# Lower rates for the gathered experts' steps in the dense products, and a higher one for their end

## The chip, the cores and the metric

The kernel runs on one core of a Trainium2 chip. Each of its five engines takes its instructions in order from a queue of its own: TensorE (PE) for matrix products, VectorE (DVE), ScalarE (ACT), GpSimd (POOL) and SyncE (SP), which here only issues transfers. The metric is device time in microseconds (us), the median of several runs. The profile is of one more execution, in which every instruction and transfer is recorded.

## The reference

The program is one layer of an encoder over 1024 tokens of width 1024: forgetting attention and an RWKV-7 state scan side by side, a gated merge, a layer norm, then a layer of product-key experts (PEER) and a second layer norm. The change lies in the expert layer alone:

```python
q = (xb @ w_q).reshape(t, PEER_HEADS, 2, PEER_HALF)
s = jnp.einsum('thpd,hpkd->thpk', q, sub_keys)
top_s, top_i = lax.top_k(s, K)                      # 16 of 128 keys, twice a head
...
best_s, best_pos = lax.top_k(cand_s.reshape(t, PEER_HEADS, K * K), K)
idx = jnp.take_along_axis(cand_i..., best_pos, axis=-1)
gate = jax.nn.softmax(best_s, axis=-1)
h = jax.nn.gelu(jnp.einsum('thkd,td->thk', u_table[idx], xb))
return jnp.einsum('thk,thkd->td', gate * h, v_table[idx])
```

Each token chooses 8 x 16 = 128 of 16384 experts. An expert is a row of 1024 floats of `u_table`, whose dot product with the token goes through a Gelu and is scaled by the gate, and a row of 1024 floats of `v_table`, which is added with that weight.

## The kernel before, in words

The 1024 tokens are eight tiles of 128. Two front passes of 512 tokens each do attention, scan, merge and the queries. For the expert layer the tiles are treated in two ways:

- **Gathered tiles** (0, 1, 2, 6, 7). The chosen rows of `u` are fetched one expert slot at a time: one indirect transfer on POOL's queue brings 128 rows, one for each token of the tile (`g<-u,eidx`, line 1389, tile `g`, five buffers, three ahead), and one DVE instruction makes the 128 dot products (line 1394, into `hh`). This is `experts_in`. After 128 slots come Gelu and gate, and `hh` is stored to `cijd` (line 1402). Then the `v` rows: the indices are loaded and turned by PE (`prepare`, lines 1664 to 1677), and one indirect transfer brings the 128 experts of one token (`v,ve`, line 1689) into a place, either one of seven buffers `vr` or a freed piece of the tile `C`. At most eight such rows are on their way once there are more than eight places. PE multiplies two rows at a time into `pg` with a window `win` that selects the token's line. This is the class `Rows`; a step of it uses two rows.
- **Dense tiles** (3, 4, 5). All 16384 experts are multiplied with the 384 tokens. The weight matrix `C` is built first from one-hot products, and then a loop over 128 columns of 128 experts does for column j: the hidden products of column j + 1 (`b<-x,u`, 24 matmuls), Gelu and weight (`csplit`), and the value products of column j (`v<-v,c`, 18 matmuls). A column loads 512 KB of `ut` (`uraw`) and 512 KB of `vt` (`vraw`) through SP's queue. Both are split into a high part on ACT (`uh`, `vh`) and a low part (`ul`, `vl`), of which POOL makes half and DVE half. Every four columns three transfers of 256 KB bring back pieces of `C` (`C<-cd`).

The steps of the gathered tiles are woven into PE's program when the kernel is built. Each matmul that is written "ticks" two background queues, `V` (the value steps) and `B` (top-k and dot products), with its nominal time times a rate; a queue hands out steps until its credit is used up:

```python
def tick(self, us):
    ...
    self.credit += us * self.rate
    while self.q and self.credit > 0:
        c = self._step()
        ...
        self.credit -= c
```

A dot-product slot costs 1.46 of credit, a value step 3.0; in the dense loop the value steps come in pairs (four rows for 6.0). The rates are constants: the first number of `RATEB` and `RATEV` holds while `C` is built, the second in the loop over the columns, and the third of `RATEV` from the column on in which the dot products of tile 7, the last gathered one, are done:

```python
g.B.rate, g.V.rate = RATEB[1], RATEV[1]
...
if f"g{GATHERED[-1]}" in g.B.done:
    g.V.rate = RATEV[2]
```

When the value steps of a gathered tile are done, `finals` adds them to the residual, does its layer norm and stores it, spread over some six columns. The dense tiles' norm follows the last column.

Of the kernel before, what the change touches and what calls it, by code (L numbers as in the profile page):

```python
# [27 lines left out]
TKI = 1  # L28
RATEP = (1, 1, 0.9)

RATEB = (2.1, 0.56)
RATEV = (4.2, 0.62, 0.95)
SEL = (1, 2, 3)
DENSE = (3, 4, 5)
GATHERED = (0, 1, 2, 6, 7)
# [321 lines left out]
def run(gen):  # L357
    for _ in gen:
        pass
# [1051 lines left out]
def dense_block(g, C):  # L1411
# [60 lines left out]

    g.B.rate, g.V.rate = RATEB[0], RATEV[0]
    zx = ExitStack()
# [6 lines left out]
    with tc.tile_pool(name="bp", bufs=BLEAD + 1) as bp, tc.tile_pool(name="cj", bufs=2) as cj:  # L1481
# [35 lines left out]
        run(xt)  # L1517
    g.B.rate, g.V.rate = RATEB[1], RATEV[1]
    u_hl, v_hl, c_hl, phs = {}, {}, {}, {}
# [95 lines left out]
    for j in range(128):  # L1615
# [11 lines left out]
        if f"g{GATHERED[-1]}" in g.B.done:  # L1627
            g.V.rate = RATEV[2]
        if j == 126:
# [218 lines left out]
```

## Time and profile before

| what | value |
|---|---|
| median of 3 runs | 3764.48 us (3761.63 to 3774.47) |
| the profiled execution | 3778.05 us, its span 3776.3 us |
| mean granted clock of TensorE | 0.921 |
| PE busy | 3261.2 us, 86% of the span |
| DVE, POOL, ACT busy | 2322.0, 2250.1, 1241.0 us |
| moved by transfers | 1019.61 MB, mean 270 GB/s |
| indirect transfers on POOL | 640 of `u` rows, 640 of `v` rows |

How to read it: a busy PE includes matmuls that overlap, since they are pipelined, so its share does not say how near to its peak it is. The DMA share is that of the 16 transfer engines. In rows of the windows view each stretch shows, for each engine, busy time and number of instructions. "Idle before" is time in which the engine did nothing ahead of the group named, with what ended it; "issue" stands for a wait that nothing in the profile explains. A queue's name has a q (SPq, POOLq).

### The profile page before, as it was taken

To read this page: it belongs to the slowest core of one execution; us is meant where nothing else is said; L and a number is where in the kernel's file an instruction comes from. 1 tells how busy PE (TensorE), PEld (TensorE's weight loads), DVE (VectorE), ACT (ScalarE), POOL (GpSimd) and SP (SyncE) were. 2 spreads that over 40 slices of the span, in tenths; PEclk is the share of its full clock that TensorE was granted. 3 is DMA by queue.
4 is the path that set the end of the run, shared out by engine and by line. 5 is a ranking of instruction groups with operands and counts; after the bars stand their busy time and mean duration, and the time that the engine had idled before them with its cause. 6 is when DMAs were issued, how large, how long until landed. Compare 5 with 4: busy or idle time off the path is not lost. (4 is left out here: it accounts for less than half of the span.)

```text
span 3776.3 us, 55545 instructions
## 1 busy us (share of the span) xinstructions
PE 3261.2 (86%) x20656; PEld 2345.8 (62%) x20656; DVE 2322.0 (61%) x5125; ACT 1241.0 (33%) x2530; POOL 2250.1 (60%) x1752
## 2 busy tenths in 40 slices
PE   7899999989987777777788677999888988999998
PEld 5577767865565555556533323777666766777787
DVE  3235333468898998898588753776656665632233
ACT  3442222334442121222344332333323332333343
POOL 2032125327576566777566565888878888866632
PEclk9899999999888778899899888999999999999999
DMA  4121124558787677878699999999999999999962
GB/s 141 51 90 44 50 93 148 176 163 297 234 274 243 232 251 269 297 252 280 209 389 392 347 365 366 370 367 380 382 363 396 392 373 374 384 335 371 353 214 98
DMA packets 338127, 1019.61 MB, mean 270 GB/s; under 512 B 46272, under 2 KB 84928, under 8 KB 336064
## 3 DMA queue, kind: packets, MB, share of 16 engines
q0 software_dynamic: 184320, 671.17, 48.2%
q1 hardware_dynamic: 141424, 324.11, 24.4%
q10 hardware_dynamic: 12112, 20.78, 1.5%
q8 instruction: 162, 2.65, 0.3%
q14 instruction: 109, 0.89, 0.1%
HBM read 960.81 MB, written 55.12 MB: 269 GB/s over the span
## 5 line engine op out<-in xcount | busy, mean ns | idle before, releaser
L1394 DVE CUSTOM_DVE_ANT_0 g<-g,ext 128x1024 f32<-128x1024 f32 x640 | 877.9, 1379 | 256.6 <-DMA g<-u,eidx 255.3
L1389 POOL DMA_INDIRECT g<-u,eidx x640 | 794.0, 1241 | 400.7 <-DVE hh L1394 107.9
L295 POOL TENSOR_TENSOR wl<-wraw,wh 128x1024 fp32r<-128x1024 f32 x131 | 322.9, 2465 | 503.5 <-ACT wh L294 459.8
L1689 POOL DMA_INDIRECT vr<-v,ve x430 | 463.3, 1078 | 192.6 <-issue 95.8
L277 PE MATMUL pg<-vr,win 128*32 128x512 f32 x1720 | 343.5, 638 | 81.3 <-DMA vr<-v,ve 79.1
L277 PE MATMUL b<-xh,uh 128*128 128x384 f32 x1024 | 356.8, 348 | 28.4 <-DVE C L1574 28.0
L277 PE MATMUL b<-xh,ul 128*128 128x384 f32 x1024 | 355.9, 348 | 27.7 <-POOL ul L295 27.7
L277 PE MATMUL b<-xl,uh 128*128 128x384 f32 x1024 | 354.1, 346 | 0.0
L277 PE MATMUL v<-vl,ch 128*128 128x512 f32 x768 | 308.2, 401 | 33.3 <-POOL vl L295 19.3
L294 ACT CAST wh<-wraw 128x1024 fp32r<-128x1024 f32 x150 | 157.3, 1048 | 503.8 <-PE pj L277 278.7
L277 PE MATMUL pj<-xh,wh 128*128 128x512 f32 x624 | 290.2, 465 | 20.9 <-ACT xh L294 7.0
L277 PE MATMUL v<-vh,cl 128*128 128x512 f32 x768 | 304.7, 397 | 0.0
L277 PE MATMUL v<-vh,ch 128*128 128x512 f32 x768 | 304.6, 397 | 0.0
L294 ACT CAST uh<-uraw 128x512 fp32r<-128x512 f32 x256 | 158.6, 621 | 370.0 <-PE b L277 327.5
L1689 POOL DMA_INDIRECT C<-v,ve x210 | 225.1, 1072 | 82.9 <-issue 52.1
L277 PE MATMUL pj<-xh,wl 128*128 128x512 f32 x624 | 261.4, 419 | 7.1 <-DVE wl L295 4.7
L277 PE MATMUL pj<-xl,wh 128*128 128x512 f32 x624 | 262.9, 421 | 2.3 <-DVE xl L295 2.2
L295 POOL TENSOR_TENSOR ul<-uraw,uh 128x512 fp32r<-128x512 f32 x128 | 169.3, 1323 | 152.4 <-ACT uh L294 146.3
L277 PEld LDWEIGHTS b<-xh,uh 128*128 128x128 f32 x1024 | 197.7, 193 | 57.2 <-DVE C L1574 35.4
L294 ACT CAST vh<-vraw 128x512 fp32r<-128x512 f32 x256 | 157.1, 620 | 215.4 <-PE v L277 163.9
L277 PEld LDWEIGHTS b<-xh,ul 128*128 128x128 f32 x1024 | 197.5, 193 | 47.4 <-POOL ul L295 32.9
L277 PEld LDWEIGHTS b<-xl,uh 128*128 128x128 f32 x1024 | 197.9, 193 | 20.3 <-issue 15.9
(353 smaller groups left out, 6466.2 us busy)
## 6 DMA issues: line engine op xcount, KB each, us to landing
wraw<-w SPq DMA_DIRECT2D x150, 512.0 KB, 3.4
uraw<-ut SPq DMA_DIRECT2D x128, 512.0 KB, 6.6
vraw<-vt SPq DMA_DIRECT2D x128, 512.0 KB, 6.7
cd<-S SPq DMA_DIRECT2D x12, 1344.0 KB, 8.4
C<-cd SPq DMA_DIRECT2D x63, 256.0 KB, 7.0
g<-u,eidx POOLq DMA_INDIRECT x640, 6.7
gtd<-tmp ACTq DMA_DIRECT2D x32, 256.0 KB, 2.3
g<-gtd SPq DMA_DIRECT2D x32, 256.0 KB, 3.4
```

The lines of the kernel that those rows point to most:

```text
L277: g.pe.matmul(o, l, r, start=start, stop=stop_)
L294: g.act.copy(hi, src)
L295: (lo_eng or g.dve).tensor_sub(lo, src, hi.bitcast(F32))
L1389: pool.indirect_dma_start(out=gg, out_offset=None, in_=A["u"], in_offset=bass.IndirectOffsetOnAxis(ap=idx[:, s_:s_ + 1], axis=0))
L1394: dve.tensor_tensor_reduce(out=gg, in0=gg, in1=xt, scale=1.0, scalar=0.0, op0=OP.mult, op1=OP.add, accum_out=hh[:, k:k + 1])
L1689: g.pool.indirect_dma_start(out=place, out_offset=None, in_=g.A["v"], in_offset=bass.IndirectOffsetOnAxis(ap=self.meta[i][1][:, t:t + 1], ...
```

## The change

Four numbers change. In the loop over the columns the rate of the dot products falls from 0.56 to 0.46, that of the value steps from 0.62 to 0.52, and after the last dot product the value steps' rate is 1.25 where it was 0.95.

```diff
-RATEB = (2.1, 0.56)
-RATEV = (4.2, 0.62, 0.95)
+RATEB = (2.1, 0.46)
+RATEV = (4.2, 0.52, 1.25)
```

All engines' programs are the same up to the first columns. From there the same instructions stand in other places. Three places show it.

POOL's queue in columns 88 to 90, from the low part `ul` of one column to that of the second after it (`g` rows are dot-product gathers, `vr` and `C` rows value gathers; x2 means two alike in a row). Before:

```order
L295 TENSOR_TENSOR ul<-uraw,uh 128x512
L295 TENSOR_TENSOR vl<-vraw,vh 128x512
L1689 DMA C<-v,ve 128x1024 x2
L1689 DMA vr_14988<-v,ve 128x1024
L1689 DMA vr_14989<-v,ve 128x1024
L295 TENSOR_TENSOR ul<-uraw,uh 128x512
L295 TENSOR_TENSOR vl<-vraw,vh 128x512
L1689 DMA vr_14987<-v,ve 128x1024
L1689 DMA C<-v,ve 128x1024 x3
L295 TENSOR_TENSOR ul<-uraw,uh 128x512
```

And after:

```order
L295 TENSOR_TENSOR vl<-vraw,vh 128x512
L1389 DMA g<-u,eidx 128x1024
L1689 DMA vr_14990<-v,ve 128x1024
L1689 DMA vr_14984<-v,ve 128x1024
L1689 DMA vr_14985<-v,ve 128x1024
L1689 DMA vr_14986<-v,ve 128x1024
L1389 DMA g<-u,eidx 128x1024
L295 TENSOR_TENSOR ul<-uraw,uh 128x512
L1389 DMA g<-u,eidx 128x1024
L295 TENSOR_TENSOR vl<-vraw,vh 128x512
L1389 DMA g<-u,eidx 128x1024 x2
L295 TENSOR_TENSOR ul<-uraw,uh 128x512
```

The dot products, which were done by column 84, now reach these columns, and fewer value gathers stand there.

POOL's queue in columns 112 to 114. Before:

```order
L295 TENSOR_TENSOR ul<-uraw,uh 128x512
L295 TENSOR_TENSOR vl<-vraw,vh 128x512
L295 TENSOR_TENSOR ul<-uraw,uh 128x512
L295 TENSOR_TENSOR vl<-vraw,vh 128x512
L295 TENSOR_TENSOR ul<-uraw,uh 128x512
```

And after:

```order
L295 TENSOR_TENSOR vl<-vraw,vh 128x512
L1689 DMA vr_14984<-v,ve 128x1024
L1689 DMA vr_14985<-v,ve 128x1024
L1689 DMA vr_14986<-v,ve 128x1024
L1689 DMA vr_14988<-v,ve 128x1024
L295 TENSOR_TENSOR ul<-uraw,uh 128x512
L1689 DMA vr_14989<-v,ve 128x1024
L1689 DMA C<-v,ve 128x1024 x3
L295 TENSOR_TENSOR vl<-vraw,vh 128x512
L1689 DMA C<-v,ve 128x1024 x2
L1689 DMA vr_14987<-v,ve 128x1024
L1689 DMA vr_14990<-v,ve 128x1024
```

Where no gather stood, two columns now have twelve.

PE where the indices of tile 7 are turned (line 1671). Before, in column 84:

```order
L277 MATMUL v_18303<-vh,ch 128x512
L277 MATMUL v_18303<-vl,ch 128x512
L1671 MATMUL b<-base,C 128x128 x3
L277 MATMUL pg<-vr_14985,win 32x512
L277 MATMUL pg<-vr_14990,win 32x512
```

And after, in column 101:

```order
L277 MATMUL v_18302<-vh,ch 128x512
L277 MATMUL pg<-vr_14988,win 32x512
L277 MATMUL pg<-vr_14989,win 32x512
L277 MATMUL pg<-vr_14988,win 32x512
L277 MATMUL pg<-vr_14989,win 32x512
L1671 MATMUL b<-base,C 128x128 x3
L277 MATMUL pg<-C,win 32x512 x4
L277 MATMUL v_18302<-vl,ch 128x512
```

Ahead of the transposes there are now two more of tile 6's last rows (`pg`), so fewer of them are left behind, ahead of tile 7's first.

## Prediction

> **What bounds the kernel now.** I read the page's forty slices first, to find where engines and transfers are full, then cut the stretch that the two numbers rule into stages, then asked each stage what it moved and what PE and POOL did in it. The change touches nothing ahead of the dense products; they begin at about 2340 us, so slice 25 of 40 on (94.4 us each).
>
> ```profile
> span 3776.3 us, 55545 instructions
> PE   7899999989987777777788677999888988999998
> POOL 2032125327576566777566565888878888866632
> PEclk9899999999888778899899888999999999999999
> DMA  4121124558787677878699999999999999999962
> GB/s 141 51 90 44 50 93 148 176 163 297 234 274 243 232 251 269 297 252 280 209 389 392 347 365 366 370 367 380 382 363 396 392 373 374 384 335 371 353 214 98
> ```
>
> From slice 25 the DMA engines are full (9) up to slice 38; slices 39 and 40 move 214 and 98 GB/s. So transfers bind for most of the products and lie idle at their end, while PE stands at 8 to 9 in the full part. The stages, cut where the value products of columns 0, 12, 80, 108 and 127 begin (columns of time, PE, PEld, DVE, ACT, POOL busy, then clock, DMA share, GB/s):
>
> ```profile
> 2353.00:2479.00 126.00, 123.44 (x652) 95.10 (x651) 91.48 (x218) 43.52 (x91) 104.71 (x84) 1.00 0.97 357
> 2479.00:3282.00 803.00, 719.85 (x3726) 551.07 (x3724) 509.13 (x724) 259.79 (x538) 672.99 (x548) 0.96 1.00 379
> 3282.00:3592.00 310.00, 305.48 (x1706) 225.58 (x1707) 96.63 (x136) 110.46 (x242) 207.82 (x194) 0.99 0.96 356
> 3592.00:3754.00 162.00, 162.00 (x840) 141.74 (x839) 52.77 (x81) 65.89 (x118) 54.83 (x45) 1.00 0.47 161
> ```
>
> Four stages, 1401 us. Call them A (12 columns, 10.5 us each), B (68 columns, 11.8), C (28 columns, 11.1) and D (19 columns, 8.5). B runs at DMA share 1.00 and leaves PE 83 us idle. C is PE's (305 of 310). D is PE alone, with half the transfer capacity unused. What was moved, from the DMA view of B, then C, then D (the packet line and the gathers' own queue, q0; of B also some issues with count, KB each and median us to landing):
>
> ```profile
> DMA packets 96844, 304.33 MB, mean 379 GB/s; under 512 B 9641, under 2 KB 24361, under 8 KB 96792
> q0 software_dynamic: 59163, 215.44, 69.8%
> uraw<-ut SPq DMA_DIRECT2D x68, 512.0 KB, 6.8
> g<-u,eidx POOLq DMA_INDIRECT x192, 8.3
> vr<-v,ve POOLq DMA_INDIRECT x136, 7.9
> C<-v,ve POOLq DMA_INDIRECT x84, 7.0
> ...
> DMA packets 40321, 110.26 MB, mean 356 GB/s; under 512 B 3612, under 2 KB 14748, under 8 KB 40300
> q0 software_dynamic: 19822, 72.18, 61.9%
> vr<-v,ve POOLq DMA_INDIRECT x79, 7.7
> C<-v,ve POOLq DMA_INDIRECT x54, 7.9
> ...
> DMA packets 11337, 26.10 MB, mean 161 GB/s; under 512 B 897, under 2 KB 5505, under 8 KB 11325
> ```
>
> The uraw loads, one a column, confirm the 68. B issued 192 + 136 + 84 = 412 gathers; 215.44 MB / 412 = 0.523 MB each. The rest of B is 88.9 MB / 68 = 1.31 MB a column, of C (110.26 - 72.18) / 28 = 1.36. PE's price of a column without gathered rows stands in the chain that ended last, and that of the value steps (tile pg) in the same cut of C:
>
> ```profile
> 3696.11 4.24 PE b L277 x24
> 3700.35 4.08 PE v L277 x18
> ...
> 3282.00:3592.00 310.00, 65.77 (x528) 13.95 (x528) 1.18 (x2) 0.99 0.96 356
> ```
>
> So 4.24 + 4.08 = 8.32 us a column; a gathered v row takes four of those matmuls, 528 / 4 = 132 rows, 65.77 / 132 = 0.50 us a row. Check on C: 28 x 8.32 + 65.8 = 299 of 310 us; PE needs its own sum and 4% more.
>
> POOL issues the gathers and makes half the low parts. In B, then in C (busy us, mean ns, idle before):
>
> ```profile
> L1389 POOL DMA_INDIRECT g<-u,eidx x192 | 231.6, 1206 | 53.7 <-issue 36.7 <-DMA eidx<-seld 9.7 <-DVE C L1574 1.2
> L1689 POOL DMA_INDIRECT vr<-v,ve x136 | 157.5, 1158 | 39.5 <-issue 34.4 <-DMA g<-u,eidx 1.8 <-PE b L277 1.5
> L295 POOL TENSOR_TENSOR vl<-vraw,vh 128x512 fp32r<-128x512 f32 x68 | 94.2, 1386 | 3.9 <-ACT vh L294 3.0
> L295 POOL TENSOR_TENSOR ul<-uraw,uh 128x512 fp32r<-128x512 f32 x68 | 91.1, 1339 | 8.4 <-ACT uh L294 7.2
> ...
> L1689 POOL DMA_INDIRECT vr<-v,ve x79 | 77.3, 979 | 20.7 <-issue 18.0 <-PE pg L277 0.6 <-PE b L277 0.5
> ```
>
> With its 130 us of idle before instructions, nearly all "issue" of 0.3 us, POOL's 673 us fill B to the end: POOL is a second full resource there. Both bounds fall with the number of gathers.
>
> **The change, part by part.** Neither work nor bytes change, only the column in which each gather and its use stand. Counted in the program's order, B's 68 columns hold 193 dot-product and 220 value gathers (the trace has 192 and 220), 6.1 a column, C 132 value gathers, D 8. After, I use four stages of new lengths: A' (columns 0 to 11) 22 + 30; B' (12 to 101) 205 + 244 = 449, or 5.0 a column; C' (102 to 121) 124, or 6.2; D' (122 to 126) none. The dot products end in column 101 instead of 83, the value steps in 121 instead of 111.
>
> A': 13 gathers fewer than the plan of A had. Bytes: 357 GB/s x 126 us = 45.0 MB, less 13 x 0.523 = 38.2 MB, at B's 379 GB/s 101 us. PE: 12 x 8.32 + 30 x 0.50 = 115 us, with the 4% 119.5. PE binds: 119.5, a gain of 6.5.
>
> B': 90 x 1.31 + 449 x 0.523 = 353 MB at 379 GB/s, 931 us. PE: 90 x 8.32 + 244 x 0.50 = 871, with 4% 906. POOL: in B 803 us less 68 x (1.386 + 1.339) = 185 leave 618 for 412 gathers, 1.50 us each; after, 449 x 1.50 + 90 x 2.725 = 919. Three bounds within 3%; I take the largest and 9 us for their beat: 940.
>
> C': 20 x 1.36 + 124 x 0.523 = 92.1 MB; 243 us at 379, 259 at C's 356. PE: 20 x 8.32 + 124 x 0.50 = 228, with 4% 237. POOL needs 124 x (0.979 + 0.30) + 40 x 1.34 = 212, so it has room. Between 243 and 259 I take 248, since the queues are full here as in B.
>
> D': 5 columns at D's 162 / 19 = 8.53: 43 us.
>
> The handover to tile 7. Its indices need the last dot product, then a chain:
>
> ```profile
> 3309.77 0.32 ACTq L1402 DMA_DIRECT2D cijd<-hh  x1
> 3314.12 0.33 SPq L1664 DMA_DIRECT2D C<-cijd  x1
> 3332.41 0.49 PE L1671 MATMUL b<-base,C 128*128 128x128 f32 x3
> 3334.34 0.96 POOL L1689 DMA_INDIRECT C<-v,ve  x1 [1.52 <-DVE ve L1677]
> ```
>
> The SP queue waits 4.35 us for the first store, with the next uraw and vraw loads behind it, before and after alike. From the transposes to the first gather are 1.9 us, and 7.9 to its landing (C's row), about 10 us. The new order puts the transposes ahead of the last v row of tile 6 and the first use of a tile 7 row closer behind them, some 5 us of PE's program instead of 7. Between 0 (another wait covers it) and 12 us (the whole chain, the POOL queue with it) I take 4, near the difference.
>
> Costed at nothing: the last layer norm of a gathered tile moves from columns 113 to 117 to columns 123 to 127, where DVE is a third busy (52.77 of 162); if that cover fails its two scaling steps, 2.5 us, come ahead of the end. Tile 7's top-k, stretched over 47 columns instead of 40, lies on DVE, which is 63% busy in B. The last column and the tail behind 3754 us stay.
>
> Sum: 119.5 + 940 + 248 + 43 + 4 = 1354.5 against 1401, so 46.5 us less. The profiled execution took 3778.05 us, 13.6 above the median of the runs, 3764.48; I take the gain over to the median: 3718 us.
>
> A rule that speaks against this: the Trainium skill, page "DMA: Bandwidth & Descriptors", section "Bandwidth", says that transfers between HBM and SBUF are bound by the core's share of HBM, some 358 GB/s. By it the estimate for B' is 353 MB / 358 = 986 us and the gain is gone; this trace does not agree, as B's row has 379 GB/s over 803 us. A lower rate as C's rows show it is rival 1.
>
> **The rivals.**
> (1) The rate falls to 356 GB/s, what C has, because traffic in B' is no longer pressed as hard: B' 353 / 0.356 = 992, C' 259, sum 119.5 + 992 + 259 + 43 + 4 = 1417, 16 more than 1401: 3780 us. For it: C's and A's rows. Against it: C waits for PE (98% busy), so 356 is what it asked for.
> (2) PE binds everywhere, since the transfers catch up in the gaps that PE's columns leave:
>
> ```profile
> 1900.00:2000.00 100.00, 87.57 (x476) 36.98 (x475) 92.47 (x434) 50.12 (x163) 64.12 (x65) 0.95 1.02 406
> ```
>
> At those 406 GB/s B' needs 870 for its bytes and PE's 906 decides; 119.5 + 906 + 237 + 43 = 1305.5, 95 us less: 3669. Against it: POOL's 919, unless its gathers fall from 1206 ns towards C's 979.
> (3) Slower: value rows come late in C'. Eight rows are on their way, so a row has two periods of four rows: before 2 x 4 / 4.71 x 11.07 = 18.8 us, after 2 x 4 / 6.2 x 12.4 = 16.0. It needs four issues of 1.28 on POOL, a split of 1.34 and 7.9 to land, 14.4. Each us beyond 16.0 costs half a us per four rows, as a wait lengthens both periods, 15 us over 31 sets. From 3 us late, landings of 12.5 us, the gain is gone; at 14 us the kernel takes some 3785. For it: the fullest queues come in these columns. Against it: C's two issue rows, 7.7 and 7.9.
>
> **How the numbers follow.** About 0.3% (11 us) is what a measurement of this kernel can tell from no change. Forecast 0.76, nearly all of it faster; rival 1 0.10, half of it within 0.3% as its rate may lie between; rival 2 0.07; rival 3 0.07, slower or the same. Faster 0.76 + 0.07 less 0.01 for the forecast's end: 0.82; same 0.09; slower 0.09. The range: downwards 28 of the 45 us by which B' at 906 and C' at 237, both PE's, lie under my terms, 3690; upwards half of rival 1's rate (B' 965, C' 254) and the handover at 12 give 3757. Outside lie about 2 in 10.
>
> **What would show it.** Dot products end at column 101; columns 12 to 101 near 10.4 us each and DMA share at 0.97 or more there; columns 102 to 121 near 12.4; only five columns at 8.3 to 8.5 with little traffic; one wait of a few us before tile 7's first rows; POOL's gathers at or under 1.2 us. Wrong it would be if B' keeps 11 us a column with DMA share under 0.95, or if PE waits for vr rows in every column of C'.

## The result: 1.8% faster, and the profile after

The changed kernel took 3700.0 us in the median of 4 runs (3689.26 to 3705.55), beside 3763.06 us for the kernel before: a ratio of 0.9824, with a 95% interval of 0.9804 to 0.9844. The forecast was 3718 us, 46 us less than before; it came out 63 us less. The profiled execution took 3689.26 us.

The page's slices of the kernel after:

```profile
span 3687.5 us, 55563 instructions
PE   7899998989987877667868867899998999999998
POOL 2031115326566556677846566688887888886773
DMA  4121124548877777877869999899999999999994
GB/s 144 52 92 45 45 96 137 189 140 283 262 262 263 243 233 247 295 259 258 309 245 397 395 343 371 337 364 361 385 383 331 392 398 396 394 396 355 403 394 164
```

The DMA engines are now full up to slice 39; before, slices 39 and 40 moved 214 and 98 GB/s, now 394 and 164. The stages of the prediction, A' to D', cut at the value products of columns 0, 12, 102, 122 and 127 (time, PE, PEld, DVE, ACT, POOL busy, clock, DMA share, GB/s):

```profile
2348.00:2462.00 114.00, 114.00 (x616) 93.45 (x615) 80.35 (x183) 42.27 (x86) 92.96 (x73) 1.00 0.92 337
2462.00:3393.00 931.00, 894.00 (x4779) 707.89 (x4778) 622.73 (x862) 337.91 (x689) 762.75 (x630) 0.99 1.00 379
3393.00:3628.00 235.00, 235.00 (x1340) 163.53 (x1339) 72.48 (x88) 81.81 (x183) 168.49 (x159) 1.00 1.00 387
3628.00:3665.00 37.00, 37.00 (x186) 33.57 (x186) 16.09 (x25) 17.24 (x29) 11.08 (x9) 1.00 0.25 86
```

They sum to 1317 us, against 1401 before. PE is busy 1280 of them, so idle for 37 us; before, it was busy 1311 and idle for 90, 83 of these in stage B alone. So of the 84 us some 53 are waits of PE that went, and 31 are the same work of PE done in less busy time; how that goes with the granted clock is told in the last section. In C' PE never waits, and the transfers run at 387 GB/s beside it.

Where the 931 us of B' go is seen on POOL (groups by line in columns 12 to 102: busy us, mean ns, idle before them):

```profile
L1389 POOL DMA_INDIRECT g<-u,eidx x200 | 238.0, 1190 | 53.2 <-issue 28.7 <-DMA eidx<-seld 10.0 <-DVE hh L1394 3.0
L1689 POOL DMA_INDIRECT vr<-v,ve x154 | 170.5, 1107 | 43.2 <-issue 37.6 <-PE v L277 1.8 <-PE b L277 0.9
L295 POOL TENSOR_TENSOR vl<-vraw,vh 128x512 fp32r<-128x512 f32 x90 | 126.3, 1403 | 9.5 <-ACT vh L294 8.4
L295 POOL TENSOR_TENSOR ul<-uraw,uh 128x512 fp32r<-128x512 f32 x90 | 119.2, 1325 | 32.1 <-ACT uh L294 30.6
L1689 POOL DMA_INDIRECT C<-v,ve x96 | 109.8, 1144 | 30.2 <-issue 25.3 <-DVE ve L1677 2.6 <-DMA g<-u,eidx 0.6
```

POOL is busy 763 us, and 92 us more go into the 0.3 us of "issue" before its gathers. Of the 76 us that are left, 49 are three waits: 30.6 and 8.4 for ACT, 10.0 for tile 7's indices. So POOL, PE (894) and the DMA engines (share 1.00) are all near full; the experiments tell which comes first.

Two single waits stand out in B'. PE's waits in columns 12 to 102 (us in all, times, longest), then what DVE and POOL did ahead of the longest, and last a wait of PE in stage B of the kernel before:

```profile
PE b L277 <- DVE C L1574: 19.0, 5, 14.2
PE v L277 <- POOL vl L295: 11.1, 18, 2.2
...
2824.47 0.94 POOL L1389 DMA_INDIRECT g<-u,eidx  x1 [9.99 <-DMA eidx<-seld]
2828.93 3.81 DVE L1394 CUSTOM_DVE_ANT_0 g<-g,ext 128x1024 f32<-128x1024 f32 x1 [11.60 <-DMA g<-u,eidx]
2832.66 0.55 DVE L1574 TENSOR_TENSOR C<-b,C 128x384 f32<-128x384 f32 x1
...
PE v L277 <- DVE vl L295: 14.0, 4, 10.9
```

When tile 6's dot products are done, tile 7's begin with a gather that waits 10 us for the indices. POOL's queue stands; DVE's next dot product waits for that gather; the weight multiply of the column (L1574) is queued behind it; and PE waits 14.2 us. The kernel before had this wait too: there the same first gather waited 9.7 us, and PE 10.9, behind a low part that DVE made late (the last line). The other wait is the handover to tile 7's value rows, column 101, which began at 3375 us. It took 18.4 us with eight value rows in it (32 matmuls into `pg`); column 103, with eight rows too, took 12.5. So the handover cost some 6 us, 3.0 of them waits of PE for the rows. The two columns, of the `pg` matmuls alone:

```profile
3374.80:3393.20 18.40, 6.34 (x32) 0.89 (x32) 0.59 (x1) 1.00 0.72 264
3403.60:3416.10 12.50, 3.85 (x32) 0.86 (x32) 0.00 (x0) 1.00 1.05 395
```

### The profile page after: what moved, and what is told of

It is laid out like the page before. It is cut to its first block, busy times and chain, and to the rows that moved or that the text cites. A ratio compares the mean times of both kernels' runs of the same rounds, so it can differ in the third digit from the quotient of the medians.

```text
span 3687.5 us, 55563 instructions
## 1 busy us (share of the span) xinstructions
PE 3232.5 (88%) x20656; PEld 2334.0 (63%) x20656; DVE 2366.5 (64%) x5125; ACT 1241.6 (34%) x2530; POOL 2243.2 (61%) x1752
## 5 line engine op out<-in xcount | busy, mean ns | idle before, releaser
L1394 DVE CUSTOM_DVE_ANT_0 g<-g,ext 128x1024 f32<-128x1024 f32 x640 | 862.5, 1356 | 165.2 <-DMA g<-u,eidx 164.1
L277 PE MATMUL pg<-vr,win 128*32 128x512 f32 x1712 | 322.4, 633 | 81.9 <-DMA vr<-v,ve 81.1
L295 DVE TENSOR_TENSOR vl<-vraw,vh 128x512 fp32r<-128x512 f32 x128 | 130.0, 1016 | 143.0 <-ACT vh L294 136.0
```

The costliest lines, as they stand in the source:

```text
L277: g.pe.matmul(o, l, r, start=start, stop=stop_)
L295: (lo_eng or g.dve).tensor_sub(lo, src, hi.bitcast(F32))
L1394: dve.tensor_tensor_reduce(out=gg, in0=gg, in1=xt, scale=1.0, scalar=0.0, op0=OP.mult, op1=OP.add, accum_out=hh[:, k:k + 1])
```

## The experiments

They ran on several chips, whose kernel before took 3796, 3767 and 3768 us in the median, so ratios to the kernel before on the same chip are compared. The changed kernel run again beside some of them:

> The changed kernel once more, on the chip of the two others: a ratio of 0.980 to 0.984 to before. Whatever they gain is counted from here.

It gave 0.9793 (0.9777 to 0.981), with 942 us in B' and 235 us in C'. So B' of the same program differs by 11 us between two profiled executions, and a difference of a stage below that tells nothing by itself.

### Each part of the change alone

Three numbers differ between the two kernels. All three runs have the higher end rate; e2 adds the slower dot products, e3 the slower value steps.

```diff
 e1:  RATEB = (2.1, 0.56)   RATEV = (4.2, 0.62, 1.25)
 e2:  RATEB = (2.1, 0.46)   RATEV = (4.2, 0.62, 1.25)
 e3:  RATEB = (2.1, 0.56)   RATEV = (4.2, 0.52, 1.25)
```

> Only the end rate of the value steps is raised (0.95 to 1.25); dot products end in column 83 as before, value steps in column 104 instead of 111. Theory 'larger of two' (each column takes the larger of its bytes at some 390 GB/s and PE's need plus 3%): the 132 late rows are PE's either way (21 columns at 11.9 us against 28 at 11.1, then 7 more columns at 8.3), so 3755 to 3765 us, no change that can be told. Theory 'idle end' (what counts is how many PE-only columns stand at the end with the transfers half idle, 5.6 us each): 7 more of them, some 3800 us.

Measured: 1.0013 (0.9993 to 1.0033). Columns 12 to 80, 80 to 104 and 104 to 127:

```profile
2504.00:3305.00 801.00, 719.74 (x3725) 554.06 (x3725) 513.03 (x729) 258.75 (x538) 669.51 (x550) 0.95 1.00 381
3305.00:3592.00 287.00, 282.81 (x1603) 197.15 (x1601) 90.88 (x120) 98.11 (x224) 204.06 (x193) 0.99 1.00 383
3592.00:3780.00 188.00, 188.00 (x952) 171.16 (x944) 60.60 (x97) 77.55 (x137) 57.30 (x45) 1.00 0.42 136
```

The last two stages took 475 us, where before they took 472 with an earlier cut. Nothing was gained by doing the late rows faster, and seven more columns with idle transfers cost nothing: "idle end" falls. PE was busy in nearly all of the last two stages (471 of 475 us), so the late rows are PE's work, in either place.

> Dot products at 0.46, value steps still at 0.62, end rate 1.25: dot products end in column 101, tile 6's value rows already in column 84, tile 7's in 122. 'Larger of two': columns 12 to 84 have 5.4 gathers each and bytes bind, 765 us; columns 84 to 101 have few and PE alone binds, 150 us; then as in the changed kernel; some 18 us over the changed kernel, 3710 to 3725 us. 'Idle end': value steps end in column 122 as in the changed kernel, so 3700 us.

Measured: 0.9928 (0.9909 to 0.9947), on the scale of 3763 us some 3736, slower than either theory said. Columns 12 to 84, 84 to 101 and 101 to 122:

```profile
2499.00:3294.00 795.00, 734.65 (x3908) 568.90 (x3907) 505.63 (x706) 275.82 (x563) 644.57 (x531) 0.98 0.98 372
3294.00:3447.00 153.00, 151.43 (x784) 131.40 (x783) 101.03 (x156) 61.56 (x112) 105.06 (x81) 1.00 0.90 323
3447.00:3710.00 263.00, 250.58 (x1399) 171.68 (x1399) 67.81 (x86) 83.56 (x195) 181.01 (x170) 0.99 0.96 359
```

The middle stage is as expected. The first took 795 us where 765 were expected. This does not tell bytes from POOL: its 296 MB at the 379 GB/s of stage B take 781 us, and the prediction's POOL prices, 389 gathers at 1.50 and 72 columns at 2.725, make 780. The last took 263. The value rows of tile 7 begin there with none on their way; PE waited for such rows four times, 8.1 of its 12 us of idle time.

> Dot products still at 0.56, value steps at 0.52 and 1.25 at the end: dot products end in column 83, value steps in column 112. 'Larger of two': columns 12 to 83 have 5.5 gathers each, 765 us, columns 83 to 111 at 11.9 us, then 15 PE-only columns; 3725 to 3745 us. 'Idle end': value steps end where they did before, so 3763 us.

Measured: 0.9942 (0.992 to 0.9965), 3741 on that scale, and in the range of "larger of two". Columns 12 to 83:

```profile
2500.00:3292.00 792.00, 724.05 (x3755) 569.43 (x3755) 527.68 (x752) 266.43 (x545) 662.23 (x533) 0.96 0.99 376
```

They took 792 us, again more than the 765 expected; POOL's prices make 781 (392 x 1.50 + 71 x 2.725), and the 298 MB at 379 GB/s make 786. So neither slower rate alone brings more than 0.7%, and the two together bring 1.8%. My reading, which no run tests by itself, is that only then do both kinds of gathers last to the same late column, so that nowhere many stand in one. The rows agree: in the stage that has both kinds of gathers PE is idle 83 us before (6.1 gathers a column), 60 in e2 (5.4), 68 in e3 (5.5) and 37 in the changed kernel (5.0).

### Which resource is full: bytes or POOL

```diff
-g.pool.indirect_dma_start(out=place, out_offset=None, in_=g.A["v"], ...
+g.pool.indirect_dma_start(out=place[:, 0:512], out_offset=None, in_=g.A["v"].rearrange("e (s c) -> (e s) c", s=2), ...
-    mm(g, po[r, :], win[...], rows[q][:, h * 512:(h + 1) * 512], m == 0, m == 31)
+    mm(g, po[r, :], win[...], rows[q][:, 0:512], m == 0, m == 31)
```

> The kernel before with half the bytes in every gathered value row: each transfer brings 512 numbers a token instead of 1024 (from the start of the table, and both halves of the product use them, so the gathered tiles' second step is not the reference's); POOL issues as many transfers, PE does as many matmuls. In columns 12 to 80 (803 us) this takes 58 of 304 MB away. Theory 'bytes bind': the stage falls to PE's need, 705 to 735 us, and the kernel by some 70 to 100 us. Theory 'POOL binds' (673 us busy and 130 us of short idle): the stage stays at 790 to 803 us.

> The same halving of the gathered value rows' bytes in the changed kernel (the second half of each row left out). Columns 12 to 102 took 931 us with 353 MB; now 289 MB. 'Bytes bind': PE's need with 3% is 897 us and some 20 us of single waits stay, so 905 to 920 us, and columns 102 to 122 stay at 235 us, PE's: 10 to 30 us in all. 'POOL binds': 925 to 935 us, nothing gained.

Both versions fetch half-rows from the first half of the table and use them for both halves of the product, so they do not compute the layer; they are there for the time alone. Columns 12 to 80 of the kernel before with half the value bytes, POOL's gathers in them, what PE waited for, and columns 12 to 102 of the changed kernel with half the value bytes:

```profile
2449.00:3245.00 796.00, 714.17 (x3722) 546.64 (x3722) 497.34 (x721) 263.68 (x537) 679.06 (x548) 0.96 0.90 310
...
L1389 POOL DMA_INDIRECT g<-u,eidx x192 | 241.9, 1260 | 50.8 <-issue 34.4 <-DMA eidx<-seld 7.3 <-DVE hh L1394 2.4
L1689 POOL DMA_INDIRECT vr<-v,ve x136 | 157.2, 1156 | 39.5 <-issue 36.0 <-DMA g<-u,eidx 2.1 <-PE b L277 0.8
...
PE b L277 <- POOL ul L295: 50.0, 22, 5.9
PE v L277 <- POOL vl L295: 22.9, 19, 3.5
...
2437.00:3357.00 920.00, 889.93 (x4782) 707.78 (x4781) 629.79 (x863) 341.71 (x690) 765.52 (x628) 0.99 0.90 312
```

A fifth of the bytes is gone, the rate falls to 310 GB/s, the DMA share to 0.90, and the stage takes 796 us instead of 803. POOL is as busy as before, and 73 of PE's 82 us of idle time are waits for the low parts that POOL makes. "Bytes bind" falls, and with it my reading of stage B in the prediction. The kernel as a whole was 0.9939 (0.9913 to 0.9964), mainly ahead of the dense products, where the same rows are fetched too: they began at 2326 us, where in e6, with all bytes and on the same chip, they began at 2351.

In the changed kernel, B' took 920 us against 931 and 942, C' 230 against 235; the ratio was 0.9701 (0.9661 to 0.974), and here too the products began earlier, at 2323 us instead of 2336 and 2348. B' came out at the upper edge of "bytes bind", 11 to 22 us shorter. As two executions of the changed kernel lie 11 us apart, bytes may have a small part by then; more is not shown.

Now POOL's load, in both directions and with the same bytes:

```diff
 e6 (before), e9 (changed):  UPOOL = (0, 0)      # all of ul on DVE
 e12 (changed):              UPOOL = (1, 1)      # all of ul on POOL
```

> The kernel before with the low parts ul all made by DVE: POOL loses one split of 1.34 us a column, DVE gains one of 0.69. 'POOL binds': columns 12 to 80 fall from 803 to 715 to 740 us. 'Bytes bind': 795 to 805 us, the same 304 MB at 379 GB/s, and the kernel is within 0.3% of before.

> The changed kernel with the low parts ul all made by DVE: POOL loses 1.3 us a column. In columns 12 to 102 (931 us) POOL was 764 us busy and 92 us in the 0.3 us steps before its gathers, and PE's need with 3% is 897. 'POOL still binds there': the stage falls to 895 to 910 us, the kernel by 20 to 35 us against the changed kernel. 'PE binds by now': 925 to 935 us, nothing gained; a loss if DVE's work comes late.

> The changed kernel with the low parts ul all made by POOL: 1.3 us a column more for POOL, 0.69 less for DVE. 'POOL binds columns 12 to 102': its spare time there was some 50 us, so the stage grows from 931 by 60 to 80 us and the kernel by as much; columns 102 to 122, where POOL has room, grow by under 10. 'Bytes or PE bind': within 10 us of the changed kernel.

Columns 12 to 80 of e6, 12 to 102 of e9 with what is left of POOL's splits there, and 12 to 102 of e12 with PE's longest waits:

```profile
2475.00:3243.00 768.00, 706.54 (x3724) 550.25 (x3723) 511.88 (x793) 257.93 (x537) 589.14 (x479) 0.96 1.02 395
...
2459.00:3376.00 917.00, 887.29 (x4778) 707.45 (x4777) 598.09 (x943) 333.27 (x690) 660.56 (x538) 0.99 1.00 383
L295 POOL TENSOR_TENSOR vl<-vraw,vh 128x512 fp32r<-128x512 f32 x90 | 157.9, 1755 | 109.5 <-ACT vh L294 108.7
...
2463.00:3467.00 1004.00, 910.59 (x4781) 711.71 (x4780) 601.84 (x772) 340.63 (x689) 869.39 (x720) 0.98 0.95 350
PE v L277 <- POOL vl L295: 43.7, 34, 4.0
PE b L277 <- POOL ul L295: 30.7, 27, 2.9
```

With less on POOL the kernel before goes from 803 to 768 us in this stage, at 395 GB/s: a ratio of 0.9915 (0.9879 to 0.9951). It stops short of the 715 to 740 expected, and the profile shows what is next: the DMA share is 1.02, and PE now waits for DVE's weight multiply, 42 us in 14 waits. The changed kernel goes from 931 and 942 to 917, a ratio of 0.975 (0.9721 to 0.9779). As a whole it is 15 us faster than the changed kernel on the same chip, between the two theories, which said 20 to 35 and nothing. POOL no longer binds there: it waits 109 us for ACT, though its other split now takes 1.76 us instead of 1.40, and PE is busy 887 of the 917 us. With more on POOL, B' grows by 62 to 73 us, as forecast from its spare time of 50 us, the rate falls to 350 GB/s, 74 of PE's 93 us of idle time are waits for POOL's low parts, and the whole gain of the change is gone: 1.0018 (0.9999 to 1.0036). C', where POOL has room, grows from 235 to 243. So POOL's queue is what stage B went by. In B' of the changed kernel POOL has little room left, but PE is nearly full beside it: 119 us more of splits on POOL cost 62 to 73 us, while as much less on POOL, or a fifth fewer bytes, brings 11 to 25 us and no more.

### The two waits, and a version that beats both kernels

```diff
+    if tile_ == 7:
+        for _ in range(4):
+            yield 1.46
     for s_ in range(128 + lead):
         ...
         if k < 0:
+            if tile_ == 7:
+                yield 1.46
             continue
 e7:  RATEB = (2.1, 0.473)  RATEV = (4.2, 0.52, 1.25)
 e8:  RATEB = (2.1, 0.495)  RATEV = (4.2, 0.51, 1.2)
 e10: e8 and UPOOL = (0, 0)
```

> The changed kernel with tile 7's dot products begun in steps (four credits of waiting after its indices are asked for, and one after each of the first three gathers; dot rate 0.473 so that they still end in column 101). In the changed kernel PE stood 14.2 us before one hidden product, behind DVE, which waited for tile 7's first dot-product rows. Theory 'that wait is lost time': it goes, 3685 to 3692 us. Rival 'bytes bind these columns anyway': the transfers use the wait, the stage stays as long, 3697 to 3703 us.

Measured: 0.9821 (0.9782 to 0.9861), no gain that can be told, and an interval that holds both theories. Columns 12 to 44, 44 to 48 and 48 to 102 of the changed kernel, then of e7:

```profile
2462.00:2784.00 322.00, 315.34 (x1695) 250.87 (x1694) 221.25 (x330) 119.91 (x243) 270.18 (x221) 0.99 0.99 374
2784.00:2839.00 55.00, 40.24 (x204) 32.82 (x203) 27.47 (x38) 13.99 (x29) 35.34 (x30) 0.88 0.93 332
2839.00:3393.00 554.00, 538.43 (x2884) 424.20 (x2884) 374.01 (x495) 204.01 (x417) 457.23 (x380) 1.00 1.01 386
...
2483.00:2813.00 330.00, 318.39 (x1697) 252.65 (x1695) 226.97 (x327) 120.30 (x243) 276.36 (x227) 0.99 0.98 372
2813.00:2851.00 38.00, 38.00 (x204) 31.61 (x204) 18.92 (x27) 14.78 (x30) 24.66 (x21) 1.00 0.92 327
2851.00:3418.00 567.00, 541.34 (x2879) 423.76 (x2878) 373.72 (x499) 202.31 (x417) 473.24 (x383) 0.99 1.00 382
```

The wait is gone, 38 us for four columns instead of 55, and the rest of the stage takes 21 us more: 935 in all against 931 and 942. As far as single executions tell, the time is given back, as the rival said, though it named the bytes. Part of it is seen on POOL: nine fewer gathers are issued in the four columns and eight more in the rest of the stage, which at the prediction's 1.50 us each is some 12 of the 21 us. The rest is not explained.

> The changed kernel with three more changes: tile 7's dot products begun in steps, dot rate 0.495, value rates 0.51 and 1.2. Dot products end in column 96, when 16 of tile 6's value rows are still to come, so that they bridge the chain to tile 7's indices. In the changed kernel that column took 18.4 us instead of 10.4. If the wait is the handover's, it goes: 8 us less than the changed kernel, a ratio of 0.978 to 0.981 to before. Rival: the faster dot products press the transfers more in columns 12 to 96 (5.1 gathers each instead of 5.0) and take it back: 0.982 to 0.984.

Measured: 0.978 (0.9744 to 0.9816), in the first theory's range. But the interval ends just short of the rival's 0.982, and beside the changed kernel's own ratios, 0.9824 and 0.9793, no gain can be told. The handover's own wait did go. The column in which tile 7's indices are turned, now column 97, took 12.8 us with eight value rows instead of 18.4 with eight, and PE did not wait in it:

```profile
3367.00:3380.00 13.00, 13.00 (x79) 8.83 (x78) 3.77 (x6) 4.77 (x13) 10.79 (x11) 1.00 1.00 397
```

> The version that bridges tile 7's start (dot rate 0.495, value rates 0.51 and 1.2, stepwise start) with the low parts ul all made by DVE. If POOL's queue is what took its gain back, both gains come: a ratio of 0.968 to 0.974 to before. If PE binds already: 0.977 to 0.980.

Measured: 3667.98 us, 0.974 (0.972 to 0.976), the fastest version here that computes the layer, and 0.5% better than the changed kernel on the same chip (0.9793). Most of that is e9's, 0.975; what the bridging adds to it can't be told.

## Why the prediction was right, by its own steps

**What bounds stage B**: wrong in the name, nearly right in the number. I read the DMA share of 1.00 as the bound and POOL as "a second full resource". Half the value bytes left B where it was (796 us), one split less on POOL made it 35 us shorter. A share of 1.00 with 379 GB/s was not the limit, since e6 moved 395. My reading of POOL's 130 us of idle time as nearly all "issue" was too high, too: the three groups of gathers have 93 us of it, 95% of the stage with POOL's busy time. The third of them, which the prediction does not show:

```profile
L1689 POOL DMA_INDIRECT C<-v,ve x84 | 100.2, 1193 | 24.7 <-issue 22.1 <-DMA g<-u,eidx 1.2 <-PE b L277 0.6
```

**A'**: 119.5 forecast, 114.4 measured. PE binds, as said, and without the 4% that I added from stage C: 12 x 8.32 + 30 x 0.50 = 115.

**B'**: 940 forecast from bytes, 931 and 942 measured. The number came out and the reason did not: e5 moved a fifth less in 920 us. That is luck, as bytes (931), POOL (919) and PE (906) lay within 3% of each other. My POOL sum with the 6 us of the handover makes 925. Its 1.50 us a gather is all of B's time that the splits leave, divided by the gathers, so it takes for granted that POOL fills B, and it holds B's own 9.7 us of waiting for tile 7's indices.

**C'**: 248 forecast, 235 measured: the term most off. I took a rate near 370 GB/s; the columns ran at 387 and PE alone set the time, 228 us by my sum and 3% more. The queues were full, at a share of 1.00; the step that failed is to take full queues for the bound.

**D'**: 43 forecast, 37.4 measured. I used the average of D, 8.53 us; but the last of these columns has no hidden products behind it, so four times 8.32 and one 4.08.

**The handover**: 4 us more than before were forecast. Measured is some 6 in the changed kernel's column 101, and some 3.5 in the kernel before, where column 85 took 13.8 us and columns with as many rows took 10.4; so the difference is some 2.5, inside the 0 to 12. The wait at tile 7's first dot product, 14.2 us, I did not name for the changed kernel, though its 9.7 us of "eidx<-seld" stood in the row that I quoted. It cost PE 10.9 us before, so it takes some 3 us from the gain; without it, in e7, no gain could be told.

**The sum**: A', C' and D' together are 24 us shorter than forecast, and B' with the handover in it 13. So in the profiled execution the four stages gained 83 us instead of 46, and the median of the runs 63: this execution is the fastest of the four, and that of before was above its median.

**The rivals**: (1), a rate of 356 GB/s, did not come: B' had 379 and C' 387. The Trainium skill, "DMA: Bandwidth & Descriptors", section "Bandwidth", has some 358 GB/s as what binds, but gives it in the same section for two cores that stream from one memory, and 425 for one core alone. This kernel runs on one core, and e6's 395 over 768 us lies above the first figure and under the second. (2), PE everywhere, came in A', C' and D', but not in B'. (3), late value rows, did not come in C', where PE has no wait at all; in e2, where tile 7's rows began with none on their way, PE waited 8.1 us for some.

## What to carry to other kernels

When two resources read full in the same stretch, take load from each by itself, with the other's unchanged, before naming the bound: here a DMA share of 1.00 hid a queue of gathers on POOL that was 95% occupied once its 0.3 us of issue per gather was counted. Where background work with a fixed total fills such a queue in some columns and leaves it idle in others, spread all kinds of it together: each of the two slower rates alone brought 0.6 to 0.7%, both 1.8%. And taking one wait of 14 us from the main engine need not bring 14 us while a queue behind it has a backlog: in e7 no gain could be told.

## What the runs showed of the hardware that I had not expected

An indirect gather of value rows occupies POOL for 1107 ns on average in B' and 983 ns in C', where DVE makes no dot products; before, it was 1158 in B and 979 in C. Halving the bytes of the value rows did not shorten it (1158 and 1156 ns in B), and in C' the transfers were as full as in B', so it is not the transfer that holds POOL. It goes with DVE: counted from the starts and ends in the trace of B', the 34 gathers during which DVE did nothing took 0.94 to 0.96 us each, and the 272 that a dot product overlapped took 1.23 on average. The other way round, a dot product of some 1.2 us took 3.81 when two of POOL's splits ran into it:

```profile
2828.20 0.94 POOL L1389 DMA_INDIRECT g<-u,eidx  x1 [0.30 <-issue]
2829.15 1.27 POOL L295 TENSOR_TENSOR ul<-uraw,uh 128x512 fp32r<-128x512 f32 x1
2830.37 1.26 POOL L295 TENSOR_TENSOR vl<-vraw,vh 128x512 fp32r<-128x512 f32 x1
2831.80 1.76 POOL L1389 DMA_INDIRECT g<-u,eidx  x1 [0.16 <-issue]
...
2828.93 3.81 DVE L1394 CUSTOM_DVE_ANT_0 g<-g,ext 128x1024 f32<-128x1024 f32 x1 [11.60 <-DMA g<-u,eidx]
```

The Trainium skill, "SBUF — State Buffer", section "SBUF: two separate sides", says that GpSimd is kept from writing a DMA's descriptors while DVE runs an operation in a mode that takes the pair of ports that the two share. The gathers fit such a lock, but no run shows whether the dot product is an operation of that kind, and no run took the dot products away, so this way of it is argued and not shown.

PE's granted clock, 0.96 in stage B, rose to 0.99 in B' with most of the gaps in PE's work gone. By the prediction's prices PE needs 674 us in B (68 x 8.32 + 216 x 0.50) and was busy 720; in B' it needs 873 (90 x 8.32 + 248 x 0.50) and was busy 894. So its busy time lay 46 us above its need in B and 21 in B', and these 25 us are most of the 31 that went. One gap shows how the two go together: after PE's wait of 14.2 us the clock was 0.68 for the next 5 us, and hidden products started every 0.32 us instead of every 0.18:

```profile
2834.00:2839.00 5.00, 5.00 (x22) 5.00 (x22) 4.41 (x8) 0.62 (x1) 1.16 (x1) 0.68 0.89 283
```

That the clock is the whole of the 25 us is not shown.
